# A two-layer decoder trunk in fp32: each weight sum held behind the DVE instruction traced before it, each DMA transpose issued half a product later behind the weight fetches traced by then

## Chip, cores and metric

The kernel runs on one NeuronCore of a Trainium2 chip. The metric is the device time of one execution in microseconds; of the kernel before there are three runs and one profiled execution.

## What is computed

Input is x of 512 tokens by 1024, a memory of 256 rows by 1024, and per-layer weights. Each of two layers is a half-step SwiGLU (1024 to 2816 to 1024), a gated token mixing of three attentions, and a second half-step SwiGLU, with RMSNorm around each. The change touches the four SwiGLU stages and, by its effect on the order, what is scheduled beside them. Cut to that:

```python
def _rmsnorm(t, g):
    t32 = t.astype(jnp.float32)
    t32 = t32 * lax.rsqrt(jnp.mean(t32 * t32, axis=-1, keepdims=True) + RMS_EPS)
    return t32.astype(t.dtype) * g

def _swiglu(t, w_gate, w_up, w_down):
    return (jax.nn.silu(t @ w_gate) * (t @ w_up)) @ w_down

mem_n = _rmsnorm(mem, mem_norm_g)
for l in range(DEPTH):
    f = _swiglu(_rmsnorm(h, ffn1_pre_g[l]), ffn1_w_gate[l], ffn1_w_up[l], ffn1_w_down[l])
    h = h + 0.5 * _rmsnorm(f, ffn1_post_g[l])
    ...
    f = _swiglu(_rmsnorm(h, ffn2_pre_g[l]), ffn2_w_gate[l], ffn2_w_up[l], ffn2_w_down[l])
    h = h + 0.5 * _rmsnorm(f, ffn2_post_g[l])
```

## The kernel before

**Arithmetic.** Every fp32 product is made of three matmuls (`mm3`, L205 to L207) on parts that TensorE reads in one pass: a weight block `raw` is copied by ACT to its high part `wh` (L182), and DVE subtracts that from `raw` to get the low part `wl` (L183). PE then multiplies wh with the high tokens, wl with the high tokens, wh with the low tokens.

**Products.** The four FFNs are called a0 and c0 in layer 0, a1 and c1 in layer 1. Sixteen of the 22 tiles of the hidden width are computed by a seven-product scheme (Strassen's in Winograd's form) over two chunks, ci = 0 and 1, first for the gate, then for the up weights, then for the down weights; the other six tiles (numbers 16 to 21) are plain and stand between the down products. The seven products run in the order 0, 2, 1, 3, 4, 5, 6. A product has two weight blocks of 512 KB, k = 0 and 2; a name such as raw_ga_1_3_0 is the block of FFN a's gate weights, chunk 1, product 3, k = 0. For the down weights the order of chunk and product is DOWN, so that down product (ci, n) = (1, 0) is followed by a plain gate and by (0, 1) and (1, 1).

**Where a weight block comes from.** `BlockUnit.fetch` (L297) has SP issue the DMA; `BlockUnit.load` (L327) has DVE make the sum or difference with a kept block t (named tga, tua, bta) for products 2, 3, 5 and 6; then comes the split. All of these are buffered in rings: two raw, eight o, four wh, four wl.

**What seeds a bank.** Product 1 adds on top of product 0's result. So ACT first copies product 0's PSUM banks into product 1's (L747 for gate and up, L878 for down), and PE's first matmul of product 1 waits for that copy. Products 2 and 3 are copied out of PSUM by ACT (L775), 4 and 5 added by DVE (L777, L784), 1, 4, 5 and 6 end with Silu (L781, L786) or with the product of gate and up (L779).

**Transposes.** A finished gate-times-up tile must be transposed before the down products. `turn(kk)` is called at each quarter of a product (kk = 0 to 3). For each of the products 1, 4, 5, 6 of an up stage, in the product after it at kk = 1, ACT copies the two 16-bit planes of the tile to th (L800), and SP issues two DMA transposes from th to tr (L801). Two or three products later, at kk = 0 and 1, ACT copies tr back into the hidden tile hr (L804). This document calls the pair for product n "Tn". The tr of products 1 and 5 has a place of its own (pool rs, a single buffer that is asked for once for each of the pair, so that the second transpose waits until the first is copied back), the others lie in a ring of five tiles. The transposes of the first up stage fall in the gate stage of ci = 1, those of the second in the down stage.

**What sets the order.** The program is traced stage by stage by a list PLAN; then a scheduler reorders each engine's instructions by priorities and modelled durations. `tc.keep_in_program_order(ins)` forbids that for one instruction: it stays behind everything that was traced before it on its engine. Every engine runs its own list strictly in order, and an instruction that waits holds up all behind it. SP's list holds the weight fetches and the transposes.

**The statistics of mem** (`mem_stats`, L1025 to L1041) are a few tiny operations on DVE and ACT in a0; ACT's four (L1036, L1037) each need a load of its function table.

Of the kernel before, what the change touches and what calls it, by code (L numbers as in the profile page):

```python
# [12 lines left out]
U16 = mybir.dt.uint16  # L13
# [5 lines left out]
P = 128  # L19
# [4 lines left out]
def kernel(  # L24
# [38 lines left out]
    nc = tc.nc  # L63
    _, S, D = x.shape
# [34 lines left out]
    def tmp(name):  # L99
        return sb.tile([P, S], F32, tag="f32t", bufs=5, name=name)  # L100
# [3 lines left out]
    def stile(shape, tag, name, dt=F32R):  # L104
        return sb.tile(shape, dt, tag=tag, bufs=BUFS[tag], name=name)
# [126 lines left out]
    class Unit:  # L232
# [19 lines left out]
        def load(self):  # L252
            if self.h is not None:
                return
            self.fetch()
            self.split_from(self.raw[:])
            self.loaded()
# [16 lines left out]
    class BlockUnit(Unit):  # L274
# [9 lines left out]
        def __init__(self, n, src, rows, k0, nk, ncol, keep, name, place="raw"):  # L284
            super().__init__(src, k0, nk, 0, ncol, name)
            self.n, self.rows, self.keep, self.fetched, self.place = n, rows, keep, False, place
            self.heir = None

        def inherits(self, un):
            un.heir, self.place = self, None  # L290
# [27 lines left out]
        def load(self):  # L318
            if self.h is not None:
                return  # L320
            self.fetch()
            src = raw = self.raw[:]
            if self.n in (2, 3, 5, 6):
                t = self.keep.get(self.k0)
                src = raw if self.n == 5 else t
                a, b = (t, raw) if self.n in (2, 5) else (raw, t)
                ins = nc.vector.tensor_tensor(src, a, b, ALU.subtract)  # L327
                if Q.pinned:
                    tc.keep_in_program_order(ins)
            self.split_from(src)  # L330
            self.loaded()
# [131 lines left out]
    Q = Queue()  # L463
# [139 lines left out]
    def ffn(l, src, wg, wu, wd, dst, name, spare, parked, plan, aside=None):  # L603
# [186 lines left out]
        def turn(kk):  # L790

            for one in turns:
                nm, g, (row, i), own, age, planes, back = one
                if kk == 1 and age == 0:
                    one[5] = planes = ([stile([P, 2, 2 * S], "rs", "tr" + nm, U16)[:, h] for h in range(2)] if own else
                                       [tmp(f"tr{nm}_{h}")[:].bitcast(U16) for h in range(2)])
                    words = g.rearrange("p f q -> p (f q)").bitcast(U16)
                    for h, plane in enumerate(planes):
                        part = tmp(f"th{nm}_{h}")[:].bitcast(U16)
                        nc.scalar.copy(part, words[:, h::2])  # L800
                        nc.sync.dma_start_transpose(plane.rearrange("p (r q) -> p r q", q=P), part)  # L801
                if kk in (0, 1) and age == back:
                    r = hidden_rows(row)[:].bitcast(U16)
                    nc.scalar.copy(r[:, :, i * S + kk:(i + 1) * S:2].rearrange("p f (e q) -> p e f q", e=2),  # L804
                                   planes[kk].rearrange("p (e f q) -> p e f q", e=2, q=P))
                if kk == ND // 2 - 1:
                    one[4] += 1
            turns[:] = [one for one in turns if one[4] <= one[6]]

        def token_products(ci, up):  # L810

            w, nm = (wu if up else wg)[l, :, ci * FC * P:(ci + 1) * FC * P], f"{'gu'[up]}{name}_{ci}"
            keep = Keep(lambda k0: stile([P, 2, S], "o", f"t{nm}_{k0}", F32)[:])
            places, had = itertools.cycle(("raw", "o", "o")), {}
            for n in ORDER:
                uns = [BlockUnit(n, w, ND // 2, k, 2, S, keep, f"{nm}_{n}_{k}", n in (2, 4) or next(places))
                       for k in range(0, ND // 2, 2)]
                if n in (2, 4):
                    for un, of in zip(uns, had[n - 2 + (n == 4)]):
                        un.inherits(of)  # L820
                had[n] = uns
                run = lambda n=n, uns=uns: token_product(ci, up, n, uns)
                early = ci == 0 and not up and n in ORDER[:4]
                yield uns, (lambda run=run: beside(run(), itertools.islice(st["some"], 1), 2)) if early else run
# [63 lines left out]
        def products():  # L888

            keep = [Keep(lambda k0, ci=ci: stile([P, 2, S], "o", f"bt{name}_{ci}_{k0}", F32)[:]) for ci in range(NC)]  # L890
            had = {}
            for at, (ci, n) in enumerate(DOWN):
                w = wd[l, ci * FC * P:(ci + 1) * FC * P]
                uns = [BlockUnit(n, w, FC // 2, k, 2, S, keep[ci], f"d{name}_{ci}_{n}_{k}", ("raw", "o")[k // 2])
                       for k in range(0, FC // 2, 2)]
                if n == 4:
                    for un, of in zip(uns, had[ci, 3]):
                        un.inherits(of)
                had[ci, n] = uns
                yield uns, (lambda at=at, uns=uns: product(at, uns))  # L900
# [804 lines left out]
```

## Time and profile before

| | us |
|---|---|
| median of three runs | 2383.31 |
| the three runs | 2377.81, 2383.31, 2385.16 |
| the profiled execution: its own time | 2377.93 |
| its span, first to last instruction | 2376.2 |
| mean granted TensorE clock of it | 0.996 of full speed |
| ACT's L804, one copy back | 1.36 |
| ACT's L800, one copy to th | 1.04 |
| DVE's L327, one weight sum | 1.22 |

Rows of the timelines below read: start in us, duration in us, engine (SPq is SP's queue of DMA issues, where the duration is that of issuing alone), line, operation, output<-inputs, shape, count, and in brackets the engine's idle time just before it and who ended that. Rows of waits read: the waiting instruction, whom it waited for, us in total, times, the longest. Rows of windows read: the window, its length, busy us and instruction count of PE, PEld, DVE, ACT and POOL, the granted clock, the DMA engines' share, GB/s.

### The profile page before, as it was taken

To read this page: it belongs to the slowest core of one execution; us is meant where nothing else is said; L and a number is where in the kernel's file an instruction comes from. 1 tells how busy PE (TensorE), PEld (TensorE's weight loads), DVE (VectorE), ACT (ScalarE), POOL (GpSimd) and SP (SyncE) were. 2 spreads that over 40 slices of the span, in tenths; PEclk is the share of its full clock that TensorE was granted. 3 is DMA by queue.
4 is the path that set the end of the run, shared out by engine and by line. 5 is a ranking of instruction groups with operands and counts; after the bars stand their busy time and mean duration, and the time that the engine had idled before them with its cause. 6 is when DMAs were issued, how large, how long until landed. Compare 5 with 4: busy or idle time off the path is not lost.

```text
span 2376.2 us, 31130 instructions
## 1 busy us (share of the span) xinstructions
PE 2347.3 (99%) x11719; PEld 1986.0 (84%) x11719; DVE 1800.1 (76%) x2358; ACT 1511.8 (64%) x2305; POOL 75.4 (3%) x134
## 2 busy tenths in 40 slices
PE   9999999999999999999999999999999999999998
PEld 7787889888888888878888878899888888888787
DVE  8876877677777688868788768766767777887785
ACT  6776465576766556774556765646777665567744
POOL 0000000000111000000000000000000100000000
PEclk9999999999999999999999999999999999999999
DMA  5666454223323555664646664542323235566743
GB/s 204 185 177 199 154 190 142 80 83 88 89 74 104 192 189 160 186 186 146 226 127 198 205 171 147 194 129 72 94 76 98 72 117 188 174 185 175 214 144 142
DMA packets 299754, 354.98 MB, mean 149 GB/s; under 512 B 78266, under 2 KB 192978, under 8 KB 299604
## 3 DMA queue, kind: packets, MB, share of 16 engines
q1 hardware_dynamic: 299508, 352.97, 48.5%
q8 instruction: 92, 1.51, 0.3%
q14 instruction: 58, 0.48, 0.1%
q0 software_dynamic: 96, 0.03, 0.0%
HBM read 319.39 MB, written 16.78 MB: 141 GB/s over the span
## 4 chain that ended last, share of the span: by engine, by line
PE 89%; DMA 3%; DVE 3%; ACT 2%; issue 1%; SPq 0%; POOL 0%; DVEq 0%; ACTq 0%
PE pg L206 4%; PE pg L207 4%; PE pg L205 4%; PE pda L206 3%; PE pdc L206 3%; PE pda L207 3%; PE pda L205 3%; PE pdc L207 2%; PE pdc L205 2%; PE pb L206 2%; PE pb L207 2%; PE pb L205 2%; PE pwo L206 1%; PE pq L206 1%; PE pq L205 1%
## 5 line engine op out<-in xcount | busy, mean ns | idle before, releaser
L205 PE MATMUL pg<-us_a,wh_wg 128*128 128x512 f32 x384 | 151.0, 393 | 0.0
L206 PE MATMUL pg<-us_a,wh_wg 128*128 128x512 f32 x384 | 149.8, 390 | 0.0
L207 PE MATMUL pg<-us_a,wl_wg 128*128 128x512 f32 x384 | 149.8, 390 | 0.0
L206 PE MATMUL pda<-wl_da,aha 128*128 128x512 f32 x224 | 89.0, 398 | 6.6 <-DVE wl_da L183 6.6
L206 PE MATMUL pdc<-wl_dc,ahc 128*128 128x512 f32 x224 | 88.7, 396 | 6.1 <-DVE wl_dc L183 6.1
L183 DVE TENSOR_TENSOR wl_da<-raw_da,wh_da 128x1024 fp32r<-128x1024 f32 x50 | 60.8, 1223 | 37.4 <-ACT wh_da L182 37.3
L205 PE MATMUL pda<-wh_da,aha 128*128 128x512 f32 x224 | 88.2, 397 | 0.8 <-ACT wh_da L182 0.5
L207 PE MATMUL pda<-wh_da,ala 128*128 128x512 f32 x224 | 88.4, 395 | 0.0
L183 DVE TENSOR_TENSOR wl_dc<-raw_dc,wh_dc 128x1024 fp32r<-128x1024 f32 x50 | 60.9, 1222 | 35.8 <-ACT wh_dc L182 35.8
L207 PE MATMUL pdc<-wh_dc,alc 128*128 128x512 f32 x224 | 87.9, 393 | 0.0
L205 PE MATMUL pdc<-wh_dc,ahc 128*128 128x512 f32 x224 | 87.4, 393 | 0.4 <-ACT wh_dc L182 0.4
L207 PEld LDWEIGHTS pg<-us_a,wl_wg 128*128 128x128 f32 x384 | 72.1, 188 | 15.2
L205 PEld LDWEIGHTS pg<-us_a,wh_wg 128*128 128x128 f32 x384 | 72.1, 188 | 14.1
L206 PEld LDWEIGHTS pg<-us_a,wh_wg 128*128 128x128 f32 x384 | 72.2, 188 | 14.1
L182 ACT CAST wh_da<-raw_da 128x1024 fp32r<-128x1024 f32 x50 | 52.1, 1049 | 41.1 <-PE pda L207 11.1
L186 DVE SCALAR_TENSOR_TENSOR wl_wg<-raw_wg,wh_wg 128x1024 fp32r<-128x1024 f32 x48 | 58.4, 1221 | 23.0 <-ACT wh_wg L185 23.0
L182 ACT CAST wh_dc<-raw_dc 128x1024 fp32r<-128x1024 f32 x50 | 52.1, 1047 | 35.3 <-DMA raw_dc<-in_ffn_w_down_dram 11.5
L200 DVE SCALAR_TENSOR_TENSOR ga<-pg,bgate,ga 128x512 f32<-128x512 f32 x48 | 35.9, 747 | 48.7 <-ACT ga L199 48.7
L182 ACT CAST wh_uc<-raw_uc 128x1024 fp32r<-128x1024 f32 x44 | 46.4, 1054 | 37.6 <-PE pwc0g L207 8.6
L185 ACT ACTIVATE wh_wg<-raw_wg 128x1024 fp32r<-128x1024 f32 x48 | 50.5, 1057 | 25.5 <-PE pv L1096 11.7
L183 DVE TENSOR_TENSOR wl_uc<-raw_uc,wh_uc 128x1024 fp32r<-128x1024 f32 x44 | 53.7, 1220 | 16.7 <-ACT wh_uc L182 16.6
L182 ACT CAST wh_ua<-raw_ua 128x1024 fp32r<-128x1024 f32 x44 | 46.2, 1052 | 28.7 <-PE pga L206 7.2
(647 smaller groups left out, 8057.2 us busy)
## 6 DMA issues: line engine op xcount, KB each, us to landing
raw_da<-in_ffn_w_down_dram SPq DMA_DIRECT2D x66, 512.0 KB, 4.9
raw_dc<-in_ffn_w_down_dram SPq DMA_DIRECT2D x66, 512.0 KB, 3.8
raw_ga<-in_ffn_w_gate_dram SPq DMA_DIRECT2D x52, 512.0 KB, 4.7
raw_ua<-in_ffn_w_up_dram SPq DMA_DIRECT2D x52, 512.0 KB, 4.6
raw_gc<-in_ffn_w_gate_dram SPq DMA_DIRECT2D x52, 512.0 KB, 4.1
raw_uc<-in_ffn_w_up_dram SPq DMA_DIRECT2D x52, 512.0 KB, 4.2
raw_wg<-in_w_gate_dram SPq DMA_DIRECT2D x48, 512.0 KB, 3.5
raw_wo<-in_w_out_dram SPq DMA_DIRECT2D x24, 512.0 KB, 3.6
```

What stands on the lines that cost most here:

```text
L182: both = [nc.scalar.copy(h_ap, src)]
L183: make = lambda: nc.vector.tensor_tensor(l_ap, src, h_ap.bitcast(F32), ALU.subtract)
L185: both = [nc.scalar.activation(h_ap, src, AF.Copy, scale=scale)]
L186: make = lambda: nc.vector.scalar_tensor_tensor(l_ap, src, scale, h_ap.bitcast(F32), ALU.mult, ALU.subtract)
L200: nc.vector.scalar_tensor_tensor(t, z, minus, t, ALU.max, ALU.add)
L205: nc.tensor.matmul(pt, lh, rh, start=start, stop=False, skip_group_check=free)
L206: nc.tensor.matmul(pt, lh, rl, start=False, stop=False, skip_group_check=free)
L207: nc.tensor.matmul(pt, ll, rh, start=False, stop=stop, skip_group_check=free)
```

## The change

Two things. First, every weight sum of the seven-product scheme (L327) is now held in program order: it stays behind all that was traced before it on DVE, above all behind the split of the block before it. Second, the transposes: the copies to th stay at kk = 1, but tr is allocated and the two DMAs issued at kk = 3, half a product later, and each of them is held on SP behind all weight fetches traced by then. The copies back stay where they were traced. No instruction is added or removed; the lines behind the edits are numbered 3 to 7 higher (L804 becomes L807, L801 becomes L804, L800 becomes L798, L1036 becomes L1043).

```diff
--- before.py
+++ after.py
@@ -284,7 +284,7 @@
         def __init__(self, n, src, rows, k0, nk, ncol, keep, name, place="raw"):
             super().__init__(src, k0, nk, 0, ncol, name)
             self.n, self.rows, self.keep, self.fetched, self.place = n, rows, keep, False, place
-            self.heir = None
+            self.heir, self.behind = None, False
 
         def inherits(self, un):
             un.heir, self.place = self, None
@@ -325,7 +325,7 @@
                 src = raw if self.n == 5 else t
                 a, b = (t, raw) if self.n in (2, 5) else (raw, t)
                 ins = nc.vector.tensor_tensor(src, a, b, ALU.subtract)
-                if Q.pinned:
+                if Q.pinned or self.behind:
                     tc.keep_in_program_order(ins)
             self.split_from(src)
             self.loaded()
@@ -792,13 +792,16 @@
             for one in turns:
                 nm, g, (row, i), own, age, planes, back = one
                 if kk == 1 and age == 0:
-                    one[5] = planes = ([stile([P, 2, 2 * S], "rs", "tr" + nm, U16)[:, h] for h in range(2)] if own else
-                                       [tmp(f"tr{nm}_{h}")[:].bitcast(U16) for h in range(2)])
+                    one[5] = planes = [tmp(f"th{nm}_{h}")[:].bitcast(U16) for h in range(2)]
                     words = g.rearrange("p f q -> p (f q)").bitcast(U16)
                     for h, plane in enumerate(planes):
-                        part = tmp(f"th{nm}_{h}")[:].bitcast(U16)
-                        nc.scalar.copy(part, words[:, h::2])
-                        nc.sync.dma_start_transpose(plane.rearrange("p (r q) -> p r q", q=P), part)
+                        nc.scalar.copy(plane, words[:, h::2])
+                if kk == 3 and age == 0:
+                    one[5] = ([stile([P, 2, 2 * S], "rs", "tr" + nm, U16)[:, h] for h in range(2)] if own else
+                              [tmp(f"tr{nm}_{h}")[:].bitcast(U16) for h in range(2)])
+                    for plane, part in zip(one[5], planes):
+                        tc.keep_in_program_order(
+                            nc.sync.dma_start_transpose(plane.rearrange("p (r q) -> p r q", q=P), part))
                 if kk in (0, 1) and age == back:
                     r = hidden_rows(row)[:].bitcast(U16)
                     nc.scalar.copy(r[:, :, i * S + kk:(i + 1) * S:2].rearrange("p f (e q) -> p e f q", e=2),
@@ -815,6 +818,8 @@
             for n in ORDER:
                 uns = [BlockUnit(n, w, ND // 2, k, 2, S, keep, f"{nm}_{n}_{k}", n in (2, 4) or next(places))
                        for k in range(0, ND // 2, 2)]
+                for un in uns:
+                    un.behind = True
                 if n in (2, 4):
                     for un, of in zip(uns, had[n - 2 + (n == 4)]):
                         un.inherits(of)
@@ -893,6 +898,8 @@
                 w = wd[l, ci * FC * P:(ci + 1) * FC * P]
                 uns = [BlockUnit(n, w, FC // 2, k, 2, S, keep[ci], f"d{name}_{ci}_{n}_{k}", ("raw", "o")[k // 2])
                        for k in range(0, FC // 2, 2)]
+                for un in uns:
+                    un.behind = True
                 if n == 4:
                     for un, of in zip(uns, had[ci, 3]):
                         un.inherits(of)
```

Since a scheduler places all that is not held, more moves than the diff names. Three places, all in a0.

ACT around the seed copies of the second gate stage (ga_1 are its weights, ua_0 and tha0u, tra0u belong to the first up stage). Before:

```order
L182 COPY wh_ga_1_2_2_1080<-tga_1_2_943 128x1024
L800 COPY tha0u_5_1_1107<-sa_0_11_591 128x1024
L804 COPY hra_1_890<-tra0u_4_1_1050 128x2x4x128
L182 COPY wh_ga_1_1_0_1122<-raw_ga_1_1_0_945 128x1024
L804 COPY hra_1_890<-tra0u_5_1102 128x2x4x128
L182 COPY wh_ga_1_1_2_1126<-raw_ga_1_1_2_1031 128x1024
L747 COPY pwa0g_1_0_1219<-pwa0g_0_0_1086 128x512
L800 COPY tha0u_6_0_1188<-sa_0_10_843 128x1024
L747 COPY pwa0g_1_1_1220<-pwa0g_0_1_1087 128x512
```

T4's second copy back and T5's first stand around the first half of product 1's split, and the first seed copy L747 is right behind its second half. Now:

```order
L798 COPY tha0u_5_0_1102<-sa_0_11_591 128x1024
L182 COPY wh_ga_1_1_2_1126<-raw_ga_1_1_2_1031 128x1024
L798 COPY tha0u_5_1_1103<-sa_0_11_591 128x1024
L807 COPY hra_1_890<-tra0u_4_0_1065 128x2x4x128
L807 COPY hra_1_890<-tra0u_4_1_1066 128x2x4x128
L798 COPY tha0u_6_0_1186<-sa_0_10_843 128x1024
L182 COPY wh_ga_1_3_0_1161<-tga_1_0_941 128x1024
L798 COPY tha0u_6_1_1187<-sa_0_10_843 128x1024
L775 COPY sa_1_11_1206<-pwa0g_2_0_1170 128x512
L775 COPY sa_1_11_1206<-pwa0g_2_1_1171 128x512
L747 COPY pwa0g_1_0_1219<-pwa0g_0_0_1086 128x512
L747 COPY pwa0g_1_1_1220<-pwa0g_0_1_1087 128x512
```

The same list now has two copies to th, the split of product 3, the copies back of T4 (L807), the copies to th of T6 and both copies out of product 2 (L775) between product 1's split and the first L747, and none of T5's copies back ahead of it.

DVE around down product (1,1) (asa and ala are sums and low parts of the tokens' side, bta_0_0 and bta_0_2 the kept blocks of product (0,2)). Before:

```order
L838 TENSOR_TENSOR asa_0_2_1926<-hra_0_931,hra_1_890 128x1024
L183 TENSOR_TENSOR wl_da_0_1_2_1777<-raw_da_0_1_2_1732,wh_da_0_1_2_1776 128x1024
L327 TENSOR_TENSOR bta_0_0_1772<-bta_0_0_1772,raw_da_0_2_0_1774 128x1024
L327 TENSOR_TENSOR bta_0_2_1780<-bta_0_2_1780,raw_da_0_2_2_1782 128x1024
L183 TENSOR_TENSOR wl_da_1_1_0_1827<-raw_da_1_1_0_1738,wh_da_1_1_0_1826 128x1024
L183 TENSOR_TENSOR ala_0_2_1925<-asa_0_2_1926,aha_0_2_1924 128x1024
L838 TENSOR_TENSOR asa_1_2_1996<-hra_2_1533,hra_3_1492 128x1024
L183 TENSOR_TENSOR wl_da_1_1_2_1833<-raw_da_1_1_2_1740,wh_da_1_1_2_1832 128x1024
```

Both sums of product (0,2) stand ahead of the split wl_da_1_1_0. Now:

```order
L843 TENSOR_TENSOR asa_0_2_1926<-hra_0_931,hra_1_890 128x1024
L183 TENSOR_TENSOR wl_da_1_1_0_1827<-raw_da_1_1_0_1738,wh_da_1_1_0_1826 128x1024
L183 TENSOR_TENSOR ala_0_2_1925<-asa_0_2_1926,aha_0_2_1924 128x1024
L845 TENSOR_TENSOR asa_0_2_1926<-asa_0_2_1926,hra_0_931 128x1024
L183 TENSOR_TENSOR wl_da_1_1_2_1833<-raw_da_1_1_2_1740,wh_da_1_1_2_1832 128x1024
L327 TENSOR_TENSOR bta_0_0_1772<-bta_0_0_1772,raw_da_0_2_0_1774 128x1024
L843 TENSOR_TENSOR asa_1_2_1996<-hra_2_1533,hra_3_1492 128x1024
L183 TENSOR_TENSOR wl_da_0_2_0_1864<-bta_0_0_1772,wh_da_0_2_0_1863 128x1024
L327 TENSOR_TENSOR bta_0_2_1780<-bta_0_2_1780,raw_da_0_2_2_1782 128x1024
```

The split of (1,1) and its second half come first, and each of the two sums stands just behind the split traced before it.

ACT around gate product (0,5), where the statistics of mem now are. Before:

```order
L781 ACTIVATE sa_0_00_637<-pwa0g_1_1_605 128x512
L182 COPY uha_4_615<-x11a_425 128x1024
L182 COPY wh_ga_0_5_0_641<-raw_ga_0_5_0_382 128x1024
L182 COPY wh_ga_0_5_2_654<-raw_ga_0_5_2_389 128x1024
L775 COPY sa_0_01_686<-pwa0g_0_0_522 128x512
L775 COPY sa_0_01_686<-pwa0g_0_1_523 128x512
L182 COPY wh_ua_0_0_0_689<-raw_ua_0_0_0_518 128x1024
L182 COPY wh_ua_0_0_2_693<-raw_ua_0_0_2_520 128x1024
```

Here the splits of (0,5) come directly behind uha_4, and no table load is near. Now:

```order
L182 COPY uha_4_615<-x11a_425 128x1024
L775 COPY sa_0_01_686<-pwa0g_0_0_522 128x512
L1043 ACT_TABLE_LOAD
L1043 ACTIVATE mem_rstd<-mem_rstd 128x1
L775 COPY sa_0_01_686<-pwa0g_0_1_523 128x512
L1044 ACT_TABLE_LOAD
L1044 ACTIVATE mem_rstd<-mem_rstd 128x1
L1043 ACT_TABLE_LOAD
L1043 ACTIVATE mem_rstd<-mem_rstd 128x1
L1044 ACT_TABLE_LOAD
L1044 ACTIVATE mem_rstd<-mem_rstd 128x1
L182 COPY wh_ga_0_5_0_641<-raw_ga_0_5_0_382 128x1024
```

Four table loads with their ACTIVATEs stand ahead of the split of (0,5); before, they stood some twelve instructions later, among the splits of the first up stage.

## The prediction

> **What bounds the kernel now.** I read the busy shares first, then who waited for whom, then the stretches around the waits, and last the engines' timelines there.
>
> ```profile
> PE 2347.3 (99%) x11719; PEld 1986.0 (84%) x11719; DVE 1800.1 (76%) x2358; ACT 1511.8 (64%) x2305; POOL 75.4 (3%) x134
> ```
>
> TensorE is busy nearly all the time. What a new order can win is TensorE's waits and the clock it loses after them; what it can lose is new waits. The longest waits of PE:
>
> ```profile
> PE pda L206 <- DVE wl_da L183: 6.6, 2, 4.3
> PE pdc L206 <- DVE wl_dc L183: 6.1, 2, 4.4
> ```
>
> These rows are four stalls at one place of each FFN, down product (1,1): 4.3 us in a1 and 6.6 - 4.3 = 2.3 in a0, 4.4 in c0 and 6.1 - 4.4 = 1.7 in c1, 12.7 in all. Further down in the same view stand two small ones that are easily passed over:
>
> ```profile
> PE pwc1g L205 <- ACT pwc1g L747: 0.8, 1, 0.8
> ...
> PE pwa0g L205 <- ACT pwa0g L747: 0.5, 1, 0.5
> ```
>
> Here PE waits for ACT's copy L747, which seeds the bank that gate product 1 of the second chunk (ci=1) goes on adding to. The rows say that this copy arrives just in time. The granted clock behind the four stalls (the column after the brackets of POOL):
>
> ```profile
> 219.00:226.00 7.00, 7.00 (x25) 5.60 (x24) 5.30 (x5) 1.88 (x3) 0.00 (x0) 0.76 0.48 150
> 1056.00:1063.00 7.00, 4.22 (x10) 3.35 (x11) 6.63 (x6) 0.00 (x0) 0.00 (x0) 0.52 0.57 190
> 1397.00:1405.00 8.00, 4.89 (x13) 3.86 (x14) 6.90 (x6) 0.06 (x1) 0.00 (x0) 0.57 0.68 197
> 2238.00:2245.00 7.00, 7.00 (x30) 5.53 (x31) 5.76 (x6) 3.00 (x4) 0.00 (x0) 1.00 0.47 150
> ```
>
> After 2.3 us of waiting, 7 us ran at 0.76: 7 x 0.24 = 1.7 us lost. After 4.4 and 4.3, 7 x 0.48 and 8 x 0.43 = 3.4 each. After 1.7, nothing. So the four places cost 12.7 + 1.7 + 3.4 + 3.4 = 21.2 us, the ceiling of any gain here.
>
> **Part 1, the down stage: the old cause goes, a smaller one comes.** DVE in a0:
>
> ```profile
> 209.88 1.23 DVE L183 TENSOR_TENSOR wl_da<-raw_da,wh_da 128x1024 fp32r<-128x1024 f32 x1 [0.32 <-ACT wh_da L182]
> 213.49 1.23 DVE L327 TENSOR_TENSOR bta<-bta,raw_da 128x1024 f32<-128x1024 f32 x1 [2.38 <-DMA raw_da<-in_ffn_w_down_dram]
> 216.17 1.22 DVE L327 TENSOR_TENSOR bta<-bta,raw_da 128x1024 f32<-128x1024 f32 x1 [1.46 <-DMA raw_da<-in_ffn_w_down_dram]
> 217.32 1.22 DVE L183 TENSOR_TENSOR wl_da<-raw_da,wh_da 128x1024 fp32r<-128x1024 f32 x1
> ```
>
> Two sums wait for blocks of a product that comes much later, and the split that PE needs stands behind them. In the changed order both sums stand behind that split, so this wait is gone. But ACT now has the back copies of T5 ahead of wh of product (1,1), and those of T6 ahead of its second half. The chain goes by these rows of SP and of ACT:
>
> ```profile
> 97.44 1.34 SPq L801 DMA_TRANSPOSE tra0u<-tha0u  x1
> ...
> 115.99 1.32 SPq L801 DMA_TRANSPOSE tra0u<-tha0u  x1
> ```
>
> ```profile
> 100.61 1.36 ACT L804 COPY hra<-tra0u 128x1024 uint16<-128x1024 uint16 x1 [0.56 <-DMA tra0u<-tha0u]
> ...
> 122.23 1.35 ACT L804 COPY hra<-tra0u 128x1024 uint16<-128x1024 uint16 x1 [2.06 <-DMA tra0u<-tha0u]
> 123.45 1.04 ACT L182 CAST wh_ga<-raw_ga 128x1024 fp32r<-128x1024 f32 x1
> ...
> 209.75 0.58 ACT L878 COPY pda<-pda 128x512 f32<-128x512 f32 x1
> ```
>
> A transpose takes 3.2 us from issue to its copy with little ahead of it (97.44 to 100.61) and 6.2 behind three fetches (115.99 to 122.23); an L804 frees ACT for the next after 1.22 (122.23 to 123.45). The second L878 ended at 210.3 and had an L804 ahead of it that now comes behind: the L804 of T5's first half ends again near 210.3. Only then may the second half go into the one buffer that T5 has: 210.3 + 3.2 = 213.5, copy 1.22, wh 1.05, wl 1.22: 217.0, and PE, which wanted wl some 2.4 us before the 218.5 at which it was made, waits 0.9. T6's two are issued behind it and two fetches; at a landing between 3.2 and 6.2 the second wh is 1 to 4 late, and I take 1.9, nearer the low end because the fetches are two and not three. So 2.8 per FFN, 11.2 in all. A wait of 1.9 lies between 1.7 (no clock lost) and 2.3 (one window): half of 4 x 1.7 = 3.4. New cost 14.6 against 21.2: **a gain of 6.6**, between 21.2 (nothing left) and nothing.
>
> **Part 2, the gate stage of ci=1: a new wait on the seed copy.** This is the term that decides. Before, in a0:
>
> ```profile
> 125.65 1.36 ACT L804 COPY hra<-tra0u 128x1024 uint16<-128x1024 uint16 x1 [1.17 <-DMA tra0u<-tha0u]
> 126.88 1.04 ACT L182 CAST wh_ga<-raw_ga 128x1024 fp32r<-128x1024 f32 x1
> 127.82 0.58 ACT L747 COPY pwa0g<-pwa0g 128x512 f32<-128x512 f32 x1
> ```
>
> ```profile
> 127.59 0.39 PE L207 MATMUL pwa0g<-wh_ga,ula 128*128 128x512 f32 x1
> 128.45 0.50 PE L205 MATMUL pwa0g<-wh_ga,us_x 128*128 128x512 f32 x1 [0.47 <-ACT pwa0g L747]
> ```
>
> PE wants the copy at 127.82 (0.23 behind 127.59) and gets it at 128.4. In the changed order, ACT has between wh of product (1,1)'s second half and this copy: one th copy, two L804, two th copies, a wh and the two L775, where before there was nothing. Where ACT begins that list follows from DVE and PE:
>
> ```profile
> 111.27 0.39 PE L207 MATMUL pwa0u<-wh_ua,ula 128*128 128x512 f32 x1
> ```
>
> ```profile
> 105.03 1.23 DVE L327 TENSOR_TENSOR tua<-raw_ua,tua 128x1024 f32<-128x1024 f32 x1 [0.90 <-DMA raw_ua<-in_ffn_w_up_dram]
> ...
> 113.04 1.27 DVE L777 TENSOR_TENSOR hra<-hra,pwa0u 128x512 f32<-128x512 f32 x2
> ```
>
> The sum at 105.03 (up product 6, second half) is now behind the L777 pair, which needs up product 5 complete (PE 111.27 + 0.23 = 111.5): pair 1.27, one wl and the sum at 1.14 each give 115.1, its wh ends at 116.1. From there ACT has, in order: L804 1.22, wh 0.95, L804 1.22, five wh and th at 0.95 (the spacing of 126.88 and 127.82), two L804, three wh and th, the L775 pair 1.07 (its row stands in part 3), L747 0.58. Sum: 1.22 + 0.95 + 1.22 + 4.75 + 2.44 + 2.85 + 1.07 + 0.58 = 15.1, so 131.2 without any gap. One gap is certain in kind: the second L804 reads the second half of T1, whose transpose waits for the first L804 (one buffer of their own, 117.3) and lands 3.2 to 6.2 later, at 120.5 to 123.5; ACT is ready at 118.3. Gap 2.2 to 5.2. Its fetches ahead are two, issued 2 and 3 us before it, so I take 2.5: the copy is done at **133.7**, PE waits 5.9 (3.4 without a gap, 8.6 at the longest).
>
> The order is the same in all four FFNs: 4 x 5.9 less the 1.3 already paid = 22.3. A wait of this length is nearest to the 4.4 and 4.3 that lost 3.4 of clock each: 13.6. **Loss 35.9.** It gives every split after it 5 us of slack, so the later rows of this stage, tight as they are, add nothing. Bounds: 4 x 3.4 - 1.3 + 4 x 1.7 = 19.1, and 4 x 8.6 - 1.3 + 4 x 5.1 = 53.5 (three windows each).
>
> [...]
>
> **Part 3, in a0 only: the statistics of mem.** Four table loads with their tiny ACTIVATEs move from a quiet place to ahead of wh of gate product (0,5):
>
> ```profile
> 60.33 2.18 ACT L182 CAST wh_ga<-raw_ga 128x1024 fp32r<-128x1024 f32 x2 [0.16 <-PE pwa0g L207]
> 62.53 1.07 ACT L775 COPY sa<-pwa0g 128x512 f32<-128x512 f32 x2
> ...
> 81.53 0.20 ACT L1037 ACTIVATE mem_rstd<-mem_rstd 128x1 f32<-128x1 f32 x1
> 81.75 1.28 ACT L1036 ACT_TABLE_LOAD   x1
> 83.04 0.20 ACT L1036 ACTIVATE mem_rstd<-mem_rstd 128x1 f32<-128x1 f32 x1
> ```
>
> ```profile
> 67.21 0.39 PE L205 MATMUL pwa0g<-wh_ga,uha 128*128 128x512 f32 x1
> ```
>
> One load with its ACTIVATE takes 1.51 (81.53 to 83.04). ACT is free at 60.2 for the first L775: 60.2 + 1.07 + 4 x 1.51 = 67.3, wh 1.05: 68.4, against PE's 67.21: 1.1 late. wl follows 1.22 later and is a further 1.0 late, and the second half's sum and wl behind it about 0.9: 3.0, with one clock window 1.7: **4.7**. Bounds: nothing, if DVE and PE have drifted by as much, and 7.3 with two windows and a slower start.
>
> [...]
>
> No instruction is added or removed, so bytes, matmuls and busy times stay. The other moved sums go behind splits on DVE, idle a quarter of the time, and are needed products later.
>
> **Sum.** The profiled execution took 2377.9 (its span is 2376.2): -6.6 + 35.9 + 4.7 = +34.0 gives 2411.9. The three runs of before go from 2377.8 to 2385.2 with the median at 2383.3, so the profiled one is at their low end. Between 34 on the one and 34 on the other (2417) I put the time at **2414**.
>
> **Rivals.** *Short waits* (0.17): T1's second half lands while ACT still works, PE waits 3.4 with one clock window each: 19.1 - 6.6 + 1.7 = +14, 2397. For it: DMA lands in 3.2 us when alone. Against it: the first L804 must come first. *Long waits* (0.10): the landing behind the fetches takes 6.2 as it did for 115.99; with 53.5 - 6.6 + 4.7 = +52, about 2433. *A gain* (0.07): the seed copy is in time, and the down stage keeps its gain of 6.6 to 21.2, 14 in the middle: 2369. It decides from the point where the wait and its clock loss are under 14 / 4 = 3.5 us per FFN, so a wait below about 2 us. Against it stands the 15.1 us of ACT work behind 116.1, without any gap; ACT would have to start 2 us sooner than PE ends up product 5. For it: ACT is busy 64% in all. *No effect* (0.06): buffers hold the engines where they were and the waits only change names: 2383.
>
> **How the numbers follow.** My own case has 0.60, between 2400 and 2428. Under 0.3% (7 us) a measurement here can't tell from no change. Faster: the gain, 0.07. Same: no effect and a sliver of the short waits, 0.07. Slower: 0.86. The range 2389 to 2440 leaves out the gain, no effect, and the tails of both outer cases, some 0.18.
>
> **What will show it.** Right: PE's wait for ACT L747 heads its waits, near 6 us in each of a0, c0, a1 and c1, with the granted clock near 0.5 in the 7 us behind it; the waits for wl_da and wl_dc at L206 fall from 12.7 to about half; a0 shows 2 to 3 us of waits at wh_ga and wl_ga near 67 us. Wrong: L747 waits of 2 us or less (then ACT's list starts sooner than I place it), or waits on L804's own transposes in the down stage as long as those removed.

## The result, and the profile after

| | before | after |
|---|---|---|
| median, us | 2381.10 (4 runs, 2377.81 to 2385.16) | 2421.78 (4 runs, 2418.01 to 2425.91) |
| ratio after to before | | 1.0169, 95% interval 1.0151 to 1.0187 |
| the profiled execution: its own time | 2377.93 | 2425.91 |
| its span | 2376.2 | 2424.2 |
| PE busy | 2347.3 | 2363.5 |
| span less PE busy: PE idle | 28.9 | 60.7 |
| mean granted clock | 0.996 | 0.990 |

The change costs 40.7 us by the medians; 2414 had been forecast. The two profiled executions are 48.0 apart, since the one of before is the fastest of its runs and the one of after the slowest of its own. The busy times on the page of after:

```profile
PE 2363.5 (97%) x11719; PEld 1994.0 (82%) x11719; DVE 1802.8 (74%) x2358; ACT 1513.7 (62%) x2305; POOL 75.3 (3%) x134
```

The same 11719 matmuls are busy for 16.2 us longer (2363.5 - 2347.3); most of that is clock, as shown below. (At full clock the 128x512 matmuls of `mm3` start 0.23 us apart, each with one record, as from 99.71 on in before; the two plain fp32 calls of L526 have four records, of 1.06 us and more.) PE is idle for 31.8 us more (60.7 - 28.9): those are waits. 16.2 + 31.8 = 48.0. DVE and ACT do the same work in times that differ by less than 0.2%. Every experiment below is read by these two numbers. Whom PE waited for in after (total, times, longest, in us):

```profile
PE pda L205 <- ACT wh_da L182: 6.6, 5, 3.1
PE pdc L205 <- ACT wh_dc L182: 6.5, 4, 2.5
PE pwc1g L205 <- ACT pwc1g L747: 6.4, 1, 6.4
PE pwc0g L205 <- ACT pwc0g L747: 6.2, 1, 6.2
PE pwa1g L205 <- ACT pwa1g L747: 5.9, 1, 5.9
PE pwa0g L205 <- ACT pwa0g L747: 5.8, 1, 5.8
PE pda L206 <- DVE wl_da L183: 3.1, 4, 0.8
PE mt L1056 <- DVE mraw L1049: 2.3, 2, 2.0
PE pdc L206 <- DVE wl_dc L183: 2.3, 3, 0.8
```

Against the list of before, the two rows that led it (wl_da 6.6, wl_dc 6.1) have shrunk to 3.1 and 2.3, and two rows for wh_da and wh_dc stand in their place. The seed copy L747 was at 0.5 and 0.8; now it appears once in each FFN, between 5.8 and 6.4, 24.3 in all. A wait of 2.0 for mt in a0 is new; before had one of 0.3, in layer 1.

The granted clock falls to 0.50 for stretches of 3.41 or 6.83 us. These are the three that before has up to its last matmul, in windows of before that match them (columns as before; the clock follows POOL's bracket):

```profile
220.01:223.42 3.41, 3.41 (x10) 2.68 (x9) 3.06 (x3) 0.92 (x1) 0.00 (x0) 0.50 0.82 292
1056.28:1063.11 6.83, 4.33 (x10) 3.46 (x11) 6.74 (x6) 0.00 (x0) 0.00 (x0) 0.50 0.56 187
1397.61:1404.44 6.83, 4.33 (x10) 3.46 (x11) 6.74 (x6) 0.00 (x0) 0.00 (x0) 0.50 0.71 210
```

And the nine of after, with two windows at full clock, 224 to 236 and 980 to 984.68:

```profile
69.90:73.31 3.41, 3.41 (x10) 2.67 (x9) 3.41 (x5) 3.16 (x4) 0.00 (x0) 0.50 0.90 295
134.76:141.59 6.83, 5.27 (x12) 4.18 (x13) 2.73 (x3) 6.60 (x9) 0.00 (x0) 0.50 0.66 153
224.00:236.00 12.00, 8.56 (x34) 5.87 (x34) 6.78 (x6) 6.83 (x7) 3.27 (x5) 1.00 0.68 177
342.97:346.38 3.41, 3.41 (x10) 2.65 (x9) 2.23 (x3) 0.29 (x1) 0.00 (x0) 0.50 0.51 158
980.00:984.68 4.68, 0.59 (x3) 0.17 (x1) 1.83 (x3) 4.68 (x6) 0.00 (x0) 1.00 1.09 334
984.68:991.51 6.83, 4.72 (x11) 3.77 (x12) 3.28 (x3) 6.83 (x9) 0.00 (x0) 0.50 0.55 105
1083.66:1087.07 3.41, 3.30 (x8) 2.62 (x9) 3.32 (x3) 0.91 (x2) 0.00 (x0) 0.50 0.00 0
1332.84:1339.67 6.83, 4.14 (x10) 3.27 (x11) 3.58 (x3) 6.83 (x10) 0.00 (x0) 0.50 0.60 124
1431.82:1438.65 6.83, 6.14 (x14) 4.79 (x15) 5.86 (x5) 2.27 (x3) 0.00 (x0) 0.50 0.35 99
2186.17:2193.00 6.83, 4.66 (x11) 3.70 (x12) 3.34 (x3) 6.83 (x9) 0.00 (x0) 0.50 0.62 127
2285.15:2288.56 3.41, 2.84 (x7) 2.27 (x8) 2.87 (x3) 0.91 (x2) 0.00 (x0) 0.50 0.00 0
```

In such a stretch PE loses half of its busy time (the first number behind the length); the time in which it stands still there is a wait and is counted as one. The stretches at 134.76, 984.68, 1332.84 and 2186.17 lie at the seed copies of a0, c0, a1 and c1 and lose 18.8 / 2 = 9.4 us. Those at 1083.66, 1431.82 and 2285.15 lie at the down stages of c0, a1 and c1 and lose 6.1; the down stage of a0 (224 to 236) loses nothing. The statistics of mem lose 1.7 (69.90), and the wait of mt 1.7 (342.97). That is 18.9 in after and 12.07 / 2 = 6.0 in before: 12.9 of the 16.2 us of longer busy time. The other 3.3 are busy time outside these stretches.

How the seed copy came to be late in a0 is seen on ACT in after:

```profile
123.53 1.36 ACT L807 COPY hra<-tra0u 128x1024 uint16<-128x1024 uint16 x1 [2.87 <-DMA tra0u<-tha0u]
...
127.59 1.05 ACT L182 CAST wh_ga<-raw_ga 128x1024 fp32r<-128x1024 f32 x1
128.55 1.03 ACT L798 COPY tha0u<-sa 128x1024 uint16<-128x1024 uint16 x1
129.49 2.53 ACT L807 COPY hra<-tra0u 128x1024 uint16<-128x1024 uint16 x2
131.89 1.03 ACT L798 COPY tha0u<-sa 128x1024 uint16<-128x1024 uint16 x1
132.83 1.04 ACT L182 CAST wh_ga<-tga 128x1024 fp32r<-128x1024 f32 x1
133.78 1.04 ACT L798 COPY tha0u<-sa 128x1024 uint16<-128x1024 uint16 x1
134.72 1.05 ACT L775 COPY sa<-pwa0g 128x512 f32<-128x512 f32 x2
135.67 1.07 ACT L747 COPY pwa0g<-pwa0g 128x512 f32<-128x512 f32 x2
```

The second copy back of T1 waits 2.87 for its transpose. The wh that ends at 128.6 is the second half of product 1's own weights, so the high part of its weights is ready, but eight instructions (128.55 to 135.67, without a gap) stand between it and the seed: three copies to th, the two copies back of T4, the split of product 3 and both copies out of product 2. Whether a second buffer for T1 would close the gap of 2.87 is open; it was not tried.

And in the down stage of a0, on ACT in after:

```profile
219.76 1.36 ACT L807 COPY hra<-tra0u 128x1024 uint16<-128x1024 uint16 x1
...
224.81 1.35 ACT L807 COPY hra<-tra0u 128x1024 uint16<-128x1024 uint16 x1 [2.11 <-DMA tra0u<-tha0u]
226.03 1.03 ACT L182 CAST wh_da<-raw_da 128x1024 fp32r<-128x1024 f32 x1
...
229.42 2.55 ACT L807 COPY hra<-tra0u 128x1024 uint16<-128x1024 uint16 x2 [1.86 <-DMA tra0u<-tha0u]
231.84 1.03 ACT L182 CAST wh_da<-raw_da 128x1024 fp32r<-128x1024 f32 x1
```

and on PE in after:

```profile
227.12 0.50 PE L205 MATMUL pda<-wh_da,aha 128*128 128x512 f32 x1 [0.87 <-ACT wh_da L182]
...
228.38 0.50 PE L206 MATMUL pda<-wl_da,aha 128*128 128x512 f32 x1 [0.76 <-DVE wl_da L183]
```

Twice ACT stands still before a copy back, 2.11 and 1.86 us, and the wh of down product (1,1) is behind it each time. PE waits for wh, and then once more for the wl that DVE makes from it.

### The profile page after: what moved, and what is told of

It reads as the page before. It is cut to its first block, busy times and chain, and to the rows that moved or that the text cites. A ratio compares the mean times of both kernels' runs of the same rounds, so it can differ in the third digit from the quotient of the medians.

```text
span 2424.2 us, 31051 instructions
## 1 busy us (share of the span) xinstructions
PE 2363.5 (97%) x11719; PEld 1994.0 (82%) x11719; DVE 1802.8 (74%) x2358; ACT 1513.7 (62%) x2305; POOL 75.3 (3%) x134
## 4 chain that ended last, share of the span: by engine, by line
PE 84%; ACT 6%; DMA 5%; DVE 2%; issue 1%; SPq 1%; POOL 0%; DVEq 0%; ACTq 0%
PE pg L206 4%; PE pg L207 4%; PE pg L205 4%; PE pda L206 2%; PE pda L205 2%; PE pda L207 2%; PE pdc L205 2%; PE pdc L206 2%; PE pdc L207 2%; PE pb L207 2%; PE pb L206 2%; PE pb L205 2%; PE pwo L206 1%; PE pq L205 1%; PE pq L206 1%
## 5 line engine op out<-in xcount | busy, mean ns | idle before, releaser
L183 DVE TENSOR_TENSOR wl_dc<-raw_dc,wh_dc 128x1024 fp32r<-128x1024 f32 x50 | 60.7, 1222 | 46.1 <-ACT wh_dc L182 45.7
L186 DVE SCALAR_TENSOR_TENSOR wl_wg<-raw_wg,wh_wg 128x1024 fp32r<-128x1024 f32 x48 | 58.4, 1220 | 21.9 <-ACT wh_wg L185 21.9
L200 DVE SCALAR_TENSOR_TENSOR ga<-pg,bgate,ga 128x512 f32<-128x512 f32 x48 | 35.9, 747 | 50.3 <-ACT ga L199 50.3
L183 DVE TENSOR_TENSOR wl_gc<-raw_gc,wh_gc 128x1024 fp32r<-128x1024 f32 x40 | 48.5, 1221 | 23.8 <-ACT wh_gc L182 23.5
L183 DVE TENSOR_TENSOR wl_ga<-raw_ga,wh_ga 128x1024 fp32r<-128x1024 f32 x40 | 48.5, 1221 | 22.7 <-ACT wh_ga L182 22.5
L183 DVE TENSOR_TENSOR wl_uc<-raw_uc,wh_uc 128x1024 fp32r<-128x1024 f32 x44 | 53.5, 1221 | 12.8 <-ACT wh_uc L182 12.7
```

The lines of the kernel that those rows point to most:

```text
L183: make = lambda: nc.vector.tensor_tensor(l_ap, src, h_ap.bitcast(F32), ALU.subtract)
L186: make = lambda: nc.vector.scalar_tensor_tensor(l_ap, src, scale, h_ap.bitcast(F32), ALU.mult, ALU.subtract)
L200: nc.vector.scalar_tensor_tensor(t, z, minus, t, ALU.max, ALU.add)
```

## The experiments

Ten kernels were run. Each table row is one kernel; the times of before beside them were 2381.54 for the first four, 2378.62 for the next four and 2379.99 for the last two. The last two columns are of the profiled execution (before: 28.9 and 2347.3). The times of before differ by up to 2.9 from group to group, so a difference between kernels of two groups is good to some 3 us.

| kernel | median (range), us | ratio to before (95%) | PE idle | PE busy |
|---|---|---|---|---|
| sums_only | 2388.93 (2384.48 to 2394.60) | 1.0034 (1.0022 to 1.0046) | 38.2 | 2352.4 |
| late_only | 2412.59 (2408.44 to 2416.90) | 1.0133 (1.0108 to 1.0159) | 50.3 | 2356.4 |
| down_sums_only | 2370.16 (2368.18 to 2374.05) | 0.9956 (0.9939 to 0.9973) | 23.8 | 2347.8 |
| seed | 2393.58 (2390.27 to 2398.39) | 1.0054 (1.0038 to 1.0070) | 40.9 | 2355.8 |
| token_sums_only | 2391.80 (2390.12 to 2396.69) | 1.0050 (1.0035 to 1.0066) | 39.9 | 2355.1 |
| no_sp_pin | 2389.06 (2385.81 to 2390.14) | 1.0039 (1.0025 to 1.0053) | 35.9 | 2351.4 |
| rstd | 2413.80 (2412.55 to 2415.51) | 1.0146 (1.0132 to 1.0160) | 52.0 | 2358.8 |
| down_mem | 2365.53 (2362.19 to 2368.26) | 0.9940 (0.9928 to 0.9953) | 19.2 | 2344.6 |
| late_nopin_only | 2392.67 (2386.76 to 2396.86) | 1.0051 (1.0032 to 1.0069) | 40.6 | 2349.8 |
| pin_only | 2407.48 (2405.04 to 2411.33) | 1.0115 (1.0092 to 1.0138) | 46.2 | 2359.7 |

### The two halves of the change apart

**sums_only**: the change with before's transposes, so all weight sums are held and nothing else differs.

```diff
-                if kk == 3 and age == 0:
...
-                        tc.keep_in_program_order(
-                            nc.sync.dma_start_transpose(plane.rearrange("p (r q) -> p r q", q=P), part))
+                        nc.sync.dma_start_transpose(plane.rearrange("p (r q) -> p r q", q=P), part)
```

> The transposes are as before the change; every weight sum is held behind the split traced in front of it. Theory A (the new wait on the seed copies comes from the later, held transposes, whose copies back now stand between the split and the seed copy): the waits on L747 are under 1 us each, the down stage loses its 12.7 us of waits and 8.5 us of clock, a0 keeps the 4 us around the table loads, which stand ahead of the split of gate product (0,5) here too: 2381 - 21 + 4 = 2364, within 2360 to 2372. Theory B (the sums, which now run later on DVE, delay the splits and with them the seed copy): waits on L747 of 4 to 6 us in all four FFNs stay, 2400 to 2420.

Measured 2388.93: 7.4 slower than before, outside the ranges of both theories. The waits on L747 and in the down stage went as Theory A has it: none for L747 is left, and the down stage is down to 1.0 to 1.7 per FFN. But a list of small waits has come, of which these are the largest of the gate and up stages in the waits of sums_only:

```profile
PE pwa0g L206 <- DVE wl_ga L183: 2.5, 4, 0.8
...
PE pwa1u L206 <- DVE wl_ua L183: 1.7, 2, 1.1
PE pwa0u L206 <- DVE wl_ua L183: 1.6, 2, 1.1
```

None of these stands in the waits of before. Held sums in the gate and up stages are not free.

**late_only**: the change without the two `un.behind = True`, so all sums are free and the transposes are late and held.

```diff
-                for un in uns:
-                    un.behind = True
```

> The sums are free as before the change; the transposes are half a product later and held behind the weight fetches. Theory A: five ACT instructions stand between the split of gate product (1,1) and the seed copy, so waits on L747 of 3 to 5 us in each FFN with 1.7 to 3.4 us of clock each, 19 to 34 in all; the down stage keeps both sums ahead of the split, but their blocks are fetched ahead of the transposes, so between none and all of its 21 us is gained: 2379 to 2415, middle 2395. Theory B: no wait on L747 over 1 us, and 2381 or less.

Measured 2412.59, 31 slower than before, near the top of Theory A's range: the transposes alone bring three quarters of the loss. PE waits 4.4, 4.0, 3.9 and 3.4 for the four seed copies, and the old stalls of the down stage stay (two of up to 4.3 each in the rows for wl_da and wl_dc, 8.0 and 8.5).

### The sums apart

**down_sums_only**: sums held in the down stage alone, everything else as before.

```diff
                 uns = [BlockUnit(n, w, FC // 2, k, 2, S, keep[ci], f"d{name}_{ci}_{n}_{k}", ("raw", "o")[k // 2])
                        for k in range(0, FC // 2, 2)]
+                for un in uns:
+                    un.behind = True
```

> Only the weight sums of the down products are held behind the split traced in front of them; gate and up sums and all transposes are as before. Theory A (the four stalls of before are the two sums ahead of that split and nothing else): all 12.7 us of waits and 8.5 us of clock go, and no other place changes: 2381 - 21 = 2360, within 2357 to 2365. Rival (the split's own block or ACT's part is next in line, and the stall only changes its name): a wait of 1 to 2 us stays at each place, 2366 to 2375.

Measured 2370.16: faster than before by 11.4. The stall that the first half of the change aims at is real: its 12.7 of waits fall to 0.7 to 1.1 at each of the four places, smaller than the rival had it, though the time lies in the rival's range. Two waits have come elsewhere, 3.0 for mraw and 2.4 at L578, each with a half-speed stretch of 3.4 us behind it.

**token_sums_only**: the counterpart, sums held in the gate and up stages alone.

```diff
             for n in ORDER:
                 uns = [BlockUnit(n, w, ND // 2, k, 2, S, keep, f"{nm}_{n}_{k}", n in (2, 4) or next(places))
                        for k in range(0, ND // 2, 2)]
+                for un in uns:
+                    un.behind = True
```

> Only the weight sums of the gate and up products are held; down sums and all transposes are as before. The kernel with all sums held took 2389 and the one with the down sums alone 2370. Theory A (the two edits add up): 2381 + (2389 - 2370) = 2400, within 2394 to 2406, made of the old down stalls (12.7 us of waits, up to 8.5 of clock) and about 16 us of small waits, each 0.8 to 1.5, at wl and wh of gate and up products and at the table loads, none on L747. Rival (the down stage's stall moves with the earlier order and the edits do not add): outside 2390 to 2410.

Measured 2391.80: 13.2 slower, 2 below the range expected. The timeline of DVE in token_sums_only shows what the hold does (up stage of ci = 1 in a0):

```profile
159.41 1.22 DVE L327 TENSOR_TENSOR tua<-tua,raw_ua 128x1024 f32<-128x1024 f32 x1
161.83 1.22 DVE L183 TENSOR_TENSOR wl_ua<-tua,wh_ua 128x1024 fp32r<-128x1024 f32 x1 [1.19 <-ACT wh_ua L182]
162.97 1.22 DVE L327 TENSOR_TENSOR tua<-tua,raw_ua 128x1024 f32<-128x1024 f32 x1
```

The second sum has to stand behind the first one's split, and that split waits for ACT's copy of the first sum. So DVE idles 1.19 in this turn of sum, wait and split: a block takes 3.56 (159.41 to 162.97) where two instructions of 1.14 spacing would take 2.3. In before, DVE at this place made a sum, a split of another block, and a sum:

```profile
159.51 1.23 DVE L327 TENSOR_TENSOR raw_ua<-tua,raw_ua 128x1024 f32<-128x1024 f32 x1
160.65 1.22 DVE L183 TENSOR_TENSOR wl_ua<-tua,wh_ua 128x1024 fp32r<-128x1024 f32 x1
161.91 1.22 DVE L327 TENSOR_TENSOR tua<-raw_ua,tua 128x1024 f32<-128x1024 f32 x1
```

without a gap, since a sum filled the time in which ACT copied.

### The transposes apart

**no_sp_pin**: the whole change, but the transposes aren't held on SP (they are still traced half a product later).

```diff
-                        tc.keep_in_program_order(
-                            nc.sync.dma_start_transpose(plane.rearrange("p (r q) -> p r q", q=P), part))
+                        nc.sync.dma_start_transpose(plane.rearrange("p (r q) -> p r q", q=P), part)
```

> The whole change, with the transposes traced half a product later but free on the DMA queue. Theory A (the hold behind the fetches, and not the half product, is what puts the copies back between the split and the seed copy): no wait on L747 above 1 us, no wait at wh of down product (1,1)'s second half above 1 us; what is left is the price of the held sums: near the 2389 of that kernel, 2383 to 2398. Theory B (the half product itself makes the copies late): waits on L747 of 3 us and more stay, 2405 to 2422.

Measured 2389.06, as Theory A has it: with the hold on SP the same kernel is 32.7 slower (30.2 with each kernel against the times of before beside it). The seed copies are no longer waited for, nor is down product (1,1) in any of the four FFNs. ACT at the same place of a0 in no_sp_pin:

```profile
124.11 1.35 ACT L806 COPY hra<-tra0u 128x1024 uint16<-128x1024 uint16 x1 [3.15 <-DMA tra0u<-tha0u]
...
126.27 1.99 ACT L182 CAST wh_ga<-raw_ga 128x1024 fp32r<-128x1024 f32 x2
128.17 1.06 ACT L747 COPY pwa0g<-pwa0g 128x512 f32<-128x512 f32 x2
```

ACT's gap ahead of a copy back is no shorter here (3.15 against 2.87), and product 1's second wh ends at nearly the same time (128.3 against 128.6). But the seed copy follows it at once, at 128.17 and not at 135.67. So it is ACT's list behind that wh, not the landing of a transpose, that holds the seed back: a hold on SP's list has moved an instruction on ACT's.

**pin_only**: before with the hold alone. The transposes stay where they were traced; sums are free.

```diff
-                        nc.sync.dma_start_transpose(plane.rearrange("p (r q) -> p r q", q=P), part)
+                        tc.keep_in_program_order(
+                            nc.sync.dma_start_transpose(plane.rearrange("p (r q) -> p r q", q=P), part))
```

> The kernel before, with the transposes at their old place and held on the DMA queue behind the weight fetches traced by then, and all sums free. Theory A (the hold alone does it): both copies to th of T6, the split of product 3 and a copy out of product 2 stand ahead of the seed copy, waits on L747 of 2 to 4 us in each FFN with a clock window each, the down stalls stay: 2393 to 2412. Theory B (hold and half product only hurt together): no wait on L747 above 1 us, 2375 to 2388.

Measured 2407.48, 27.5 slower than before, in Theory A's range. The waits of pin_only for the seed copies:

```profile
PE pwc1g L205 <- ACT pwc1g L747: 4.8, 1, 4.8
PE pwa0g L205 <- ACT pwa0g L747: 4.6, 1, 4.6
PE pwa1g L205 <- ACT pwa1g L747: 4.2, 1, 4.2
PE pwc0g L205 <- ACT pwc0g L747: 3.1, 1, 3.1
```

**late_nopin_only**: late_only without the hold; the transposes are half a product later and otherwise free.

```diff
-                        tc.keep_in_program_order(
-                            nc.sync.dma_start_transpose(plane.rearrange("p (r q) -> p r q", q=P), part))
+                        nc.sync.dma_start_transpose(plane.rearrange("p (r q) -> p r q", q=P), part)
```

> The kernel before, with the transposes issued half a product later but free on the DMA queue, and all sums free. Theory A (half a product later is harmless by itself): no wait on L747 above 1 us, the down stalls of before stay: 2375 to 2388. Theory B: late transposes hold ACT's copies back, 2 us and more at each seed copy, 2390 or more.

Measured 2392.67: 12.7 slower than before, in Theory B's range. The waits for seed copies are 1.4 to 2.7 in each FFN, and the stalls of the down stage stay (wl_da 7.0 in all, wl_dc 8.4, against 6.6 and 6.1 before). With sums_only and no_sp_pin beside them, the transposes give this table (medians, us; before was between 2378.6 and 2381.5 beside them):

| | at the old place | half a product later |
|---|---|---|
| sums free, not held on SP | 2380.0 (before) | 2392.7 |
| sums free, held on SP | 2407.5 | 2412.6 |
| all sums held, not held on SP | 2388.9 | 2389.1 |
| all sums held, held on SP | not run | 2421.8 |

The hold is the larger part in both orders (27.5 and 19.9 with free sums, 32.7 with held ones). The half product costs 12.7 with free sums that are not held on SP, 5.1 with the hold, and 0.1 with held sums, within the 3 us between groups: the costs do not add up. An explanation that fits, and was not tested further, is that each edit changes the order that the next one meets.

### Two repairs, and a faster kernel

**seed**: the whole change, but the seed copies of gate and up are traced at the start of product 2, which ORDER runs before product 1, and product 1's banks are taken there.

```diff
-            if n in (0, 1, 2):
+            if n in (0, 2):
                 st["c", ci, up, n] = [pbank("z" if n == 0 else "mm", f"pw{nm}_{e}") for e in range(2)]
-            if n == 1:
+            if n == 2:
+                st["c", ci, up, 1] = [pbank("mm", f"pw{nm[:-1]}1_{e}") for e in range(2)]
```

> The whole change, and the seed copies of product 1 traced one product earlier, right after product 0, with product 1's banks allocated there. Theory A (24.3 us of waits on L747 and 13.6 us of clock behind them are the price of that copy's place): 2422 - 38 = 2384, within 2380 to 2390. Rival (the copies back then delay the next splits, wh of gate products (1,3) and (1,4), which had been given slack by the stall): 2 to 4 us per FFN come back there with a clock window, 2394 to 2407.

Measured 2393.58, 28.2 below the change and inside the rival's range. Of the waits for seed copies one of 0.4 is left. Splits further on are late in their place, though not at the gate products that the rival named: each up stage of ci = 1 waits 1.7 to 2.3 for its wl, where after had at most 0.5, and the down stages keep 2.7 to 4.0 per FFN. The seed waits had hidden the smaller ones.

**rstd**: the whole change, with ACT's first logarithm of the statistics of mem held in program order.

```diff
-                nc.scalar.activation(ss[:, 1:2], ss[:, 0:1], AF.Ln)
+                tc.keep_in_program_order(nc.scalar.activation(ss[:, 1:2], ss[:, 0:1], AF.Ln))
```

> The whole change, with ACT's first operation of the memory's statistics held in program order, so that the table loads stand outside the FFN. Theory A: the 2.2 us of waits at wh and wl of gate product (0,5) and the half-speed window behind them go: 3.9 us less, 2418, within 2413 to 2421. Rival: the statistics then come late for the memory's own transposes, the wait of 2.0 us there grows by as much, and the time stays at 2422.

Measured 2413.80, 8.0 below the change (5.5 with each against the times of before beside it). The waits at gate product (0,5) are down to 0.4, and that of mt from 2.0 to 0.3. The four seed waits stay (6.4 in a0, 5.3 in c0, 5.9 in a1, 6.4 in c1). But the gain can't be put down to the table loads and mt alone: the waits for wh_da and wh_dc fell as well, from 13.1 to 7.5, and the trace has 9 table loads in place of 14, so the hold has removed loads and not only moved them.

**down_mem**: down_sums_only, with the rows of mem fetched on GpSimd's queue and not on SP's.

```diff
-            nc.sync.dma_start(raw[:], mem[0, t * P:(t + 1) * P, :])
+            nc.gpsimd.dma_start(raw[:], mem[0, t * P:(t + 1) * P, :])
```

> The down sums alone held, and the memory's two rows for the second norm fetched by GpSimd's queue and not behind the weight fetches. In the kernel with the down sums alone, the wait for these rows cost 3.0 us and half a window of 3.4, and a wait for DVE at the transposes of c0's norm 2.4 and as much. Theory A: the first goes and the second stays, 2370 - 4.7 = 2365. Rival: GpSimd's transfer is slower to start and the wait stays, 2370 or more.

Measured 2365.53, faster than before and after: 0.994 of before (0.9928 to 0.9953). The wait for mraw in a0 is gone, as Theory A has it. What that is worth in time is not shown, since the interval of the ratio overlaps that of down_sums_only (0.9939 to 0.9973). The windows of down_mem at two of the four old stalls:

```profile
1056.00:1063.00 7.00, 7.00 (x32) 5.80 (x32) 6.90 (x7) 4.97 (x6) 0.00 (x0) 1.00 0.48 150
1397.00:1405.00 8.00, 8.00 (x37) 6.63 (x36) 6.36 (x6) 3.02 (x4) 0.00 (x0) 1.00 0.54 181
```

where before had PE busy for 4.22 and 4.89 at clocks of 0.52 and 0.57. PE is idle for 19.2 in all (28.9 in before) and busy for 2344.6.

## Why the prediction was right, and where its sizes were off

**Part 2, the seed copy: right in mechanism, and in the size of the waits.** Predicted were waits of 5.9 in each FFN, 22.3 more than before; measured are 24.3 - 1.3 = 23.0. The walk along ACT's list foresaw both pieces: a gap for T1's second transpose (2.5 taken, 2.87 measured) and the work behind it. By then all of a0 ran some 2.6 us later than the walk had it (the first seed copy ended near 136.2, not 133.7): waits of 2.5 and clock of 1.7 had come at (0,5), and waits of 1.6 that before had up to there (1.1 for ula, 0.5 for the first up stage's seed) were gone. PE was as late, so the difference stayed. Named too broadly was the cause. The prediction put the new order down to the change as a whole; no_sp_pin and pin_only show that the hold on SP moves the seed copy back on ACT. Why the scheduler answers a hold on SP so was not looked into.

**Clock behind it: the length right, the price too high.** As forecast, each of the four waits brought as much half speed as the 4.4 and 4.3 of before, 6.83 us. But the prediction multiplied length by lost clock (7 x 0.48 = 3.4) and added that to the wait, though PE stands still for 1.6 to 2.7 us of each stretch; those are in the wait already. So the 13.6 became 9.4, and the 8.5 that the prediction gave to before is 6.0 in the same way.

**Part 1, the down stage: the mechanism right, the size wrong.** The step "So 2.8 per FFN, 11.2 in all" failed. Measured are 2.6 + 0.8 = 3.4 in a0, 3.4 + 0.8 = 4.2 in c0, 3.6 + 0.8 = 4.4 in a1 and 3.0 + 0.8 = 3.8 in c1: 15.8, with 6.1 of clock 21.9. Against 12.7 + 6.0 = 18.7 before there is no gain of 6.6 but a loss of 3.2. The second wh was taken 1.9 late, and in a0 it was (1.8). The first was taken as one wait of 0.9 at wl, and was two in a row, 0.87 for wh and 0.76 for wl. In the other FFNs the longest wait for wh is 2.4, 3.1 and 2.5, toward the upper end of the "1 to 4" that the prediction gave for the second wh. Three of the four places lost clock, and the 3.4 taken for it became 6.1. With before's transposes the same held sums leave 1.0 to 1.7 per FFN (sums_only), so most of the 15.8 is the transposes' part.

**Part 3, the statistics of mem: about right.** 1.4 + 1.1 = 2.5 of waits against 3.0, and 1.7 of clock as foreseen; the 1.1 for ula that before had just ahead of this place is gone, which the prediction did not count.

**Not foreseen: mt.** In a0 PE waits 2.0 at L1056, and loses 1.7 of clock. On DVE in after the reason is one row:

```profile
340.92 0.75 DVE L1049 TENSOR_SCALAR mraw<-mraw,mem_rstd 128x1024 f32<-128x1024 f32 x1 [1.17 <-DMA mraw<-in_mem_dram]
```

A row block of mem arrives late; its fetch is on SP's list, which the prediction had followed for weights and transposes alone. The wait in a0 comes with the held down sums: it is 1.6 to 3.3 in sums_only, down_sums_only, no_sp_pin, seed and after, and absent in the four kernels with free down sums (token_sums_only, late_only, late_nopin_only, pin_only). Two edits each bring it to 0.3 or less in spite of held down sums, one on ACT (rstd) and one of the queue (down_mem), so how the lateness arises is only partly known.

**Free in the prediction, but not free: the held sums of gate and up.** The step "The other moved sums go behind splits on DVE, idle a quarter of the time, and are needed products later" fails: alone they cost 13.2 (token_sums_only). It counted DVE's busy time, and the hold puts ACT's copy into DVE's chain. In the whole change this price hardly shows in the gate and up stages, because PE waits longer for the seed copy there, as the prediction had said of the later rows of the gate stage; without the hold on SP it shows again (no_sp_pin, +10.4 over its before).

**The sum, and luck in it.** For the profiled pair +34.0 was predicted and +48.0 measured. Seed 23.0 + 9.4 = 32.4 (predicted 35.9), mem 4.2 (4.7), down stage +3.2 (-6.6), mt 3.7 (0): 43.5. The 4.5 left are 3.3 of busy time outside the half-speed stretches and small waits, not assigned one by one. By the medians the change costs 40.7, since the profiled executions stand at opposite ends of their runs; the 2414 lacks 7.8. That it lacks no more is in part luck: the seed term was 3.5 too dear, and that hid a part of the 9.8 by which the down stage was too cheap and of the 3.7 for mt. One more slip touches no forecast: the rival of short waits adds 1.7 for the statistics of mem where Part 3 has 4.7; with 4.7 it stands at 2400.

## What to carry to other kernels

When an instruction is held on one queue, compare the order of every engine, not of that queue alone: here a hold on SP's list went with eight instructions ahead of a seed copy on ACT, and cost 20 to 33 us, where half a product of delay cost 13 at most. Hold only what stands in the way: the same pin that gains 11 us in the down stage costs 13 in the gate and up stages, where a sum used to fill the time of another engine's copy and where sum, copy and split now run one after the other. And the longest wait hides shorter ones behind it, so removing it (28 us) gives back less than its length and clock (24.3 + 9.4 = 33.7 us). When clock is added to waits, count only the half-speed time in which the engine works: here 4.1 to 5.3 of the 6.83 us at each seed copy.

## What the runs showed of the hardware that was not expected

The clock fell behind some short waits and not behind others. In after, 2.02 us of wait at mt were followed by 3.41 us at 0.50, and the 1.38 and 0.76 at gate product (0,5) by as much; in before, the 2.31 in a0 brought 3.41. The 1.68 in c1 of before brought none (1.00 from 2238 to 2245), nor did 1.61 at L578 in after, nor the 0.87, 0.76 and 1.76 in the down stage of a0, all between 226.25 and 232.92 (1.00 from 224 to 236).

Nor did the half speed grow in step with the wait. In the down stages of after, 2.35 in c0 and 2.54 in c1 went with 3.41 us of it, 3.06 in a1 with 6.83. The 4.41 and 4.27 of before went with 6.83 each, and so did the seed waits of after, 5.8 to 6.4. What decides between none, 3.41 and 6.83 these numbers do not show.

A transpose that had to wait for its one buffer was issued on SP at 221.14, right behind the copy that freed it (219.76 + 1.36 = 221.12), and its own copy back began at 224.81: 3.67 us from issue to use, 0.5 above the 3.2 of one with little ahead of it.
